# A spare buffer for the blocks that a triangular solve turns, and diagonal copies on three engines, in a hybrid DeltaNet and attention layer

## The chip, the core and the metric

The kernel runs on one core of a Trainium2 chip. A core has five engines that each run a queue of their own in order: TensorE (PE, matrix products; the loads of its weights are listed as PEld), VectorE (DVE), ScalarE (ACT), GpSimd (POOL) and SyncE (SP), which here issues all DMA transfers. Engines wait for each other through semaphores. The metric is the device time of one execution in microseconds; a comparison of two kernels takes the median of several runs of each.

## What is computed

One layer of a bidirectional encoder on x of 2048 rows and 1024 columns, all in float32. The rows are normalised and multiplied by one input matrix, whose columns are split between two groups that are summed at the end:

```python
h = rms_norm(x, norm_w[l])
proj = h @ w_in[l]
dn = gated_deltanet_bidir(dn_q, dn_k, dn_v, dn_beta, dn_decay, ...)   # 4 heads of 128
dn = rms_norm(dn, dn_out_norm_w[l]) * silu(dn_z)
sw = windowed_gqa_with_sinks(sw_q, sw_k, sw_v, ...) * silu(sw_z)      # 8 query heads of 64, 2 key heads
x = x + concat([dn, sw]) @ w_out[l]
```

The gated delta rule, run forward and backward, holds the part that the change touches. In each chunk a unit lower triangular matrix is inverted, and a state is carried from chunk to chunk:

```python
m = where(strict, (k_beta @ k.T) * decay, 0)
t_inv = triangular_solve(eye + m, eye)        # one per chunk
u, w = t_inv @ (v * beta), t_inv @ (k_beta * exp(g))
# scan over the chunks: v_new = u - w @ state; o = ...; state = state * exp(g_last) + k_dec.T @ v_new
```

The reference has chunks of 64; the kernel works the same recurrence in chunks of 128, 16 of them per head and direction.

## The kernel before

The first phase, until about 660 us, makes everything that comes before the recurrence: x is normalised and split into a high and a low part (three products in place of one, hence L191 to L193 and L202 to L204), the projections run, the convolution and SiLU follow (L242, L249), and the windowed attention runs beside them (L343 to L382). Its results go to DRAM: keys and queries per head (kq_d), values (v_d), gates.

The second phase runs over the four heads. Each head goes through four functions, and the work of one head lies beside the scan of the head before it:

- `pre_front(h)`, L637 to L723, in four groups of four chunks: loads keys and queries into a tile of the pool tag "kq", which has two buffers (L654), transposes them on TensorE (L674, tile tr), forms the products of keys with keys and queries (L694, tile gh), scales them on VectorE (L703, tile ma) and writes the triangular matrices to DRAM (L708, m_d).
- `solve(h)`, L725 to L746, inverts the 32 by 32 blocks on the diagonals, 128 of them on 128 partitions, by 31 pairs of VectorE steps: a product into tm (L741), a subtraction from X (L745). L holds the blocks, X starts as the unit matrix, which GpSimd writes by two memsets (L735, L736). The blocks of direction 0 have to be turned: they are loaded into X (L731) and copied, with rows and columns swapped, into L (L734), before X is overwritten. The result goes to DRAM (L746, x_d).
- `invert(h)`, L748 to L796, builds the inverses of the 128 by 128 matrices from the blocks, in four rounds `hi`, each for one group of chunks in both directions. A round loads two pieces of x_d (L757, xc), transposes them on VectorE (L758, xt), adds two matrices into g on GpSimd (L761), and places the 32 by 32 blocks on the diagonals of three operands: e1 by L763, e2 by L765, e3 by L767, four copies each, all on GpSimd. In the trace these operands are iv, and in the order iv0, iv2 and iv3. Five products on TensorE follow (L772, pi0 to pi4), with ScalarE moving their results (L781, b1; L787 to L796), and eight more copies on GpSimd (L784) that place blocks into ma.
- `scan(h)`, L798 to L853, carries the state S through 16 chunks in both directions: a product of the state with the keys (L812, pk), its difference to the values (L814, r), products with the inverse (L821, py), the state's update (L830, L833; L837 is the copy that makes the first state) and the output (L823, L839, L844 to L850, tile oacc). The output's normalisation and gate follow (L864 to L882, tiles sso, tro, zt).

Matmuls that depend on none of this fill TensorE's gaps: 32 pieces of the attention group's output product (L599 to L601, tile pcs, with mxs, mhs, mls as their operands; L602 adds a loaded tile xrs), and some late gate projections (pf_z).

No order is written out by hand. A planner at the end of the build (`set_order`, from L938) takes the instructions, their dependences, a table of costs and lags (L931, L1091) and the pools' number of buffers, runs a list schedule forward and backward twelve times, and fixes the order of all five queues. An edit of a few instructions therefore gives another order in the whole program.

## Time and profile before

| | |
|---|---|
| median of 3 runs | 1278.94 us (1277.84 to 1281.57) |
| the profiled execution | 1274.25 us, its span 1272.5 us |
| mean granted TensorE clock | 0.992 |
| PE busy | 1219.4 us (96%), 7066 matmuls |
| DVE, ACT, POOL busy | 889.5 us (70%), 703.2 us (55%), 507.4 us (40%) |
| DMA | 205.34 MB, mean 161 GB/s |

The span is the time from the first to the last instruction of the profiled execution; the 1.75 us beside it lie around them. An engine's busy time has no waits in it. A share over the whole span hides the stages: until 660 us the first phase runs, from there on the heads. A row of the timeline gives the start, the duration, the engine (SPq is SP's queue of issues), the line, the operation, the output and the inputs, how many of the same kind are taken together, and in brackets how long the engine stood idle before it and what ended that.

### The profile page before, as it was taken

What the parts mean: (1) busy time and instruction counts of PE and PEld (TensorE: products, weight loads), DVE (VectorE), ACT (ScalarE), POOL (GpSimd) and SP (SyncE); (2) the same over time, 40 slices, a digit from 0 to 9 for tenths busy, and PEclk for the clock granted to TensorE, in tenths of its full rate; (3) what the DMA queues carried; (4) which work ended last, traced back from release to release, by engine and by line L of the source; (5) the groups of instructions that cost most, each with busy time, mean ns of one, the idle gap of its engine ahead of it and who ended that gap; (6) DMA issues with size and microseconds to landing.
All of it is one profiled execution on the core that took longest, in us unless ns stands there. A gap on an engine that the chain in (4) does not pass through costs nothing.

```text
span 1272.5 us, 22253 instructions
## 1 busy us (share of the span) xinstructions
PE 1219.4 (96%) x7066; PEld 1044.4 (82%) x7066; DVE 889.5 (70%) x2154; ACT 703.2 (55%) x2105; POOL 507.4 (40%) x893
## 2 busy tenths in 40 slices
PE   6999999999999999999999998998799899999998
PEld 6998877788889998787788787887688789798876
DVE  4422387999975589999986573788488879557333
ACT  6321254776644677776654425858557955566210
POOL 1330044666613398665221306613672651641000
PEclk9999999999999999999999998999899999999999
DMA  8442254322544434522137826967965974746675
GB/s 269 145 132 76 95 180 128 97 97 81 180 132 144 130 96 116 158 87 67 58 117 244 224 96 189 276 189 207 270 169 154 269 191 138 217 145 214 227 242 205
DMA packets 225510, 205.34 MB, mean 161 GB/s; under 512 B 48497, under 2 KB 175089, under 8 KB 225393
## 3 DMA queue, kind: packets, MB, share of 16 engines
q1 hardware_dynamic: 225392, 203.92, 52.7%
q8 instruction: 56, 0.92, 0.3%
q14 instruction: 62, 0.50, 0.1%
HBM read 138.79 MB, written 65.08 MB: 160 GB/s over the span
## 4 chain that ended last, share of the span: by engine, by line
PE 67%; DVE 12%; DMA 9%; ACT 7%; issue 3%; POOL 1%; SPq 0%; DVEq 0%; ACTq 0%; POOLq 0%
PE pf_c L191 4%; PE pf_c L192 4%; PE pf_c L193 4%; PE pf_z L191 4%; PE pf_z L192 4%; PE pf_z L193 4%; PE pi L772 4%; DVE acc L242 3%; PE pt L363 3%; PE pq_q L202 2%; PE pq_q L204 2%; PE pq_q L203 2%; PE pcd L561 2%; PE pcd L563 2%; PE pcd L562 2%
## 5 line engine op out<-in xcount | busy, mean ns | idle before, releaser
L191 PE MATMUL pf_c<-xhi,wh_c 128*128 128x512 f32 x384 | 151.0, 404 | 0.7 <-DVE acc L242 0.4
L192 PE MATMUL pf_c<-xlo,wh_c 128*128 128x512 f32 x384 | 150.6, 401 | 0.0
L193 PE MATMUL pf_c<-xhi,wl_c 128*128 128x512 f32 x384 | 149.1, 401 | 0.0
L242 DVE SCALAR_TENSOR_TENSOR acc<-pf_c,cw,acc 128x512 f32<-128x512 f32 (+1 forms) x192 | 140.3, 743 | 11.3 <-ACT acc L238 9.2
L358 POOL TENSOR_SCALAR pr<-pr,st 128x384 f32<-128x384 f32 (+1 forms) x128 | 80.1, 648 | 71.3 <-DVE st L356 60.0
L191 PE MATMUL pf_z<-xhi,wh_z 128*128 128x512 f32 x256 | 86.6, 401 | 0.5 <-DVE zo L215 0.5
L349 ACT ACTIVATE pr<-pr,st 128x384 f32<-128x384 f32 (+1 forms) x128 | 76.1, 596 | 19.6 <-DVE st L345 19.1
L192 PE MATMUL pf_z<-xlo,wh_z 128*128 128x512 f32 x256 | 86.2, 399 | 0.0
L191 PEld LDWEIGHTS pf_c<-xhi,wh_c 128*128 128x128 f32 x384 | 72.1, 188 | 15.3 <-DVE acc L242 1.7
L193 PE MATMUL pf_z<-xhi,wl_z 128*128 128x512 f32 x256 | 84.7, 397 | 0.0
L192 PEld LDWEIGHTS pf_c<-xlo,wh_c 128*128 128x128 f32 x384 | 72.3, 188 | 13.0
L193 PEld LDWEIGHTS pf_c<-xhi,wl_c 128*128 128x128 f32 x384 | 71.8, 188 | 13.0
L345 DVE CUSTOM_DVE_ANT_0 pr<-s,mask,sink 128x384 f32<-128x384 f32 (+1 forms) x128 | 72.5, 593 | 12.4 <-PE s L344 8.3
L367 ACT ACTIVATE ph<-pt 128x512 fp32r<-128x512 f32 x92 | 53.0, 596 | 40.9 <-PE pt L363 39.1
L826 ACT ACTIVATE yk<-py,ck 128x128 f32<-128x128 f32 x120 | 43.9, 366 | 49.5 <-PE py L821 48.4
L363 PE MATMUL pt<-ident,pr 128*128 128x128 f32 x368 | 67.2, 274 | 1.9 <-DVE q L327 1.1
L368 DVE TENSOR_TENSOR pl<-pt,ph 128x512 fp32r<-128x512 f32 x92 | 61.6, 681 | 5.1 <-ACT ph L367 5.0
L703 DVE SCALAR_TENSOR_TENSOR ma<-gh,bp,dc 128x256 f32<-128x256 f32 x128 | 54.9, 476 | 10.4 <-PE gh L694 8.7
L363 PEld LDWEIGHTS pt<-ident,pr 128*128 128x128 f32 x368 | 46.5, 140 | 17.7 <-DVE pl L368 3.0
L202 PE MATMUL pq_q<-wh_q,xhi 128*128 128x256 f32 x256 | 60.3, 285 | 0.6 <-ACT sgkv L261 0.3
L599 PE MATMUL pcs<-wohs,mhs 128*128 128x512 f32 x128 | 57.7, 451 | 2.9 <-ACT mhs L593 2.3
L814 DVE SCALAR_TENSOR_TENSOR r<-pk,negc,vs 128x128 f32<-128x128 f32 x120 | 41.5, 346 | 27.1 <-PE pk L812 26.6
(251 smaller groups left out, 3709.8 us busy)
## 6 DMA issues: line engine op xcount, KB each, us to landing
kqc<-kq_d SPq DMA_DIRECT2D x120, 128.0 KB, 3.0
ws_c<-wt SPq DMA_DIRECT2D x48, 256.0 KB, 3.3
xr<-x SPq DMA_DIRECT2D x16, 512.0 KB, 6.3
ws_z<-wt SPq DMA_DIRECT2D x32, 256.0 KB, 3.9
kq<-kq_d SPq DMA_DIRECT2D x16, 512.0 KB, 5.3
m_d<-ma SPq DMA_DIRECT2D x32, 256.0 KB, 5.4
mxs<-mix_sw SPq DMA_DIRECT2D x32, 256.0 KB, 3.8
xrs<-x SPq DMA_DIRECT2D x32, 256.0 KB, 3.6
```

The lines of the kernel that those rows point to most:

```text
L191: T.matmul(ps, hi[:, k, cs], xhi[b][:, k], start=(k == 0), stop=False)
L192: T.matmul(ps, hi[:, k, cs], xlo[b][:, k], start=False, stop=False)
L193: T.matmul(ps, lo[:, k, cs], xhi[b][:, k], start=False, stop=(k == KC - 1))
L202: T.matmul(ps[:, :n], xh, hi[:, k, :n], start=(k == 0), stop=False)
L242: V.scalar_tensor_tensor(av, ps[:, lo:], cw[:, i, k : k + 1], av, ALU.mult, ALU.add)
L345: V.tensor_tensor_reduce(pr[j][:, :n], ps[:, :n], mask[:, lo * P : hi * P], 1.0, sink[:, hh : hh + 1], ALU.add, ALU.min, accum_out=nm[:, j ...
L349: A.activation(pr[j][:, :n], pr[j][:, :n], AF.Exp, bias=nm[:, j : j + 1], scale=-1.0, accum_out=den[:, j : j + 1])
L358: G.tensor_scalar(pr[j][:, :n], pr[j][:, :n], den[:, j : j + 1], 1.0, ALU.mult, ALU.mult)
L363: T.transpose(pt[:, j], pr[j][:, (kb - lo) * P : (kb - lo + 1) * P], ident)
L368: V.tensor_tensor(pl, ptf, ph.bitcast(F32), ALU.subtract)
L599: T.matmul(ps, mh[:, k], wh[:, k], start=(k == 0), stop=False)
L703: V.scalar_tensor_tensor(ma[d, c4][:, c], gh[:, k], bp[:, d, cc : cc + 1], gms[d][:, c : c + 1].to_broadcast([P, 2, P]), ALU.mult, ALU.mult,)
```

## The change

Two edits in `solve` and `invert`. In `solve` the blocks of direction 0 are loaded into a new tile lt, which takes a buffer of the "kq" tag, the key tiles of `pre_front`, with still two buffers for that tag. The copy into L reads lt, and stands behind the memsets in the code. In `invert` the copies into e1, e2 and e3 of round 0 go to VectorE, GpSimd and ScalarE, four each; those of rounds 1 to 3 stay on GpSimd. From here on the lines behind the edit have numbers up to three higher (L757 is L759, L758 is L760, L772 is L775; L741 and L745 are L743 and L747; the copies of e1 and e2 are L770, of e3 on ScalarE L768).

```diff
--- before.py
+++ after.py
@@ -728,12 +728,14 @@
         X = qa.tile([P, 32, 32], F32, tag="X", name=f"X{h}")
         lv = [m_d[d].rearrange("u (p y) -> (u p) y", p=4)[:, : 32 * P] for d in range(2)]
         lv = [a.rearrange("q (r x) -> q r x", x=P)[:, :, :32] for a in lv]
-        dma(X[0:64], lv[0])
+        lt = q1.tile([P, 2, 512], F32, tag="kq", name=f"lt{h}", bufs=2).rearrange("p a s -> p (a s)")
+        lt = lt.rearrange("p (r c) -> p r c", c=32)
+        dma(lt[0:64], lv[0])
         dma(L[64:128], lv[1])
         x = X.rearrange("p r c -> p (r c)")
-        V.tensor_copy(L[0:64], X[0:64].rearrange("p r c -> p c r"))
         G.memset(x, 0.0)
         G.memset(x[:, ::33], 1.0)
+        V.tensor_copy(L[0:64], lt[0:64].rearrange("p r c -> p c r"))
         for c in range(31):
             n = 31 - c
             tm = qa.tile([P, 256], F32, tag="tm", name=f"tm{h}_{c}")
@@ -759,12 +761,13 @@
                 x0[d], x1[d] = (xc, xt) if d == 0 else (xt, xc)
             g = qb.tile([P, 4, P], F32, tag="g", name=f"g{h}_{hi}", bufs=2)
             G.tensor_tensor(g, m[:, :, 0], m[:, :, 1], ALU.add)
-            for p, q in enumerate(quads):
-                G.tensor_copy(e1[q, :, q], x0[p % 2][q])
-            for p, q in enumerate(quads):
-                G.tensor_copy(e2[q, :, q], x1[1 - p % 2][q])
-            for p, q in enumerate(quads):
-                G.tensor_copy(e3[q, :, q], x0[p // 2][q])
+            for s, a, b in zip("GGG" if hi else "VGA", (e1, e2, e3), ([0, 1, 0, 1], [1, 0, 1, 0], [0, 0, 1, 1])):
+                xs = x1 if a is e2 else x0
+                for q, k in zip(quads, b):
+                    if s == "A":
+                        A.activation(a[q, :, q], xs[k][q], AF.Copy)
+                    else:
+                        (V if s == "V" else G).tensor_copy(a[q, :, q], xs[k][q])
 
             def prod(j, lhs, rhs):
                 o = ps_i[(hi + j) % 2].tile([P, 4, P], F32, tag="inv", name=f"pi{j}_{h}_{hi}")
```

The planner makes a new order of it. Places of it follow. In names such as `tm1_30_10279` the first number is the head, and the last is a running number of the tile.

VectorE at the end of solve(1), beside the last steps of scan(0) and the products of pre_front(2). Before:

```order
L741 TENSOR_TENSOR tm1_29_10274<-L1_10180,X1_10181 128x60
L685 RECIPROCAL ssk2_11259<-ssk2_11259 128x4
L849 SCALAR_TENSOR_TENSOR oacc0_0_8962<-po0_1_15_9607,egc_4915,oacc0_0_8962 128x128
L745 TENSOR_TENSOR X1_10181<-X1_10181,tm1_29_10274 128x2x30
L703 SCALAR_TENSOR_TENSOR ma2_0_11427<-gh2_0_1_11475,bp2_11261,dc2_0_0_11424 128x2x128
...
L686 TENSOR_TENSOR bp2_11261<-beta_4885,ssk2_11259 128x2x4
L741 TENSOR_TENSOR tm1_30_10277<-L1_10180,X1_10181 128x31
L703 SCALAR_TENSOR_TENSOR ma2_3_11431<-gh2_0_1_11475,bp2_11261,dc2_0_1_11428 128x2x128
L745 TENSOR_TENSOR X1_10181<-X1_10181,tm1_30_10277 128x31
L850 TENSOR_TENSOR oacc0_0_8962<-po0_1_15_9607,oacc0_0_8962 128x128
L849 SCALAR_TENSOR_TENSOR oacc0_3_8975<-po0_0_15_9592,egc_4915,oacc0_3_8975 128x128
```

After:

```order
L747 TENSOR_TENSOR X1_10182<-X1_10182,tm1_29_10276 128x2x30
L836 SCALAR_TENSOR_TENSOR S0_0_14_9561<-S0_0_13_9521,egt_4913,po0_0_14_9553 128x128
L743 TENSOR_TENSOR tm1_30_10279<-L1_10181,X1_10182 128x31
L703 SCALAR_TENSOR_TENSOR ma2_2_11279<-gh2_2_1_11399,bp2_11263,dc2_2_0_11350 128x2x128
L747 TENSOR_TENSOR X1_10182<-X1_10182,tm1_30_10279 128x31
L703 SCALAR_TENSOR_TENSOR ma2_1_11275<-gh2_2_1_11399,bp2_11263,dc2_2_1_11353 128x2x128
L817 SCALAR_TENSOR_TENSOR r0_0_15_9590<-pk0_0_15_9588,negc_4911,vs0_3_8016 128x128
L836 SCALAR_TENSOR_TENSOR S0_1_14_9581<-S0_1_13_9541,egt_4913,po0_1_14_9573 128x128
L852 SCALAR_TENSOR_TENSOR oacc0_3_8976<-po0_0_14_9553,egc_4915,oacc0_3_8976 128x128
...
L817 SCALAR_TENSOR_TENSOR r0_1_15_9605<-pk0_1_15_9603,negc_4911,vs0_0_7950 128x128
L853 TENSOR_TENSOR oacc0_0_8963<-po0_1_14_9573,oacc0_0_8963 128x128
L703 SCALAR_TENSOR_TENSOR ma2_0_11429<-gh2_0_0_11466,bp2_11263,dc2_0_0_11426 128x2x128
```

The last step of solve(1), X1 from tm1_30, stood behind the L703 steps on gh2_0_0 and gh2_0_1 and the scan's r0_0_15, S0_1_14 and r0_1_15; now these stand behind it.

TensorE at the first product of the inverse of head 1, pi0_1_0. Before:

```order
L694 MATMUL gh2_3_0_11540<-kq2_3_11498 128x256 x2
L694 MATMUL gh2_3_1_11551<-kq2_3_11498 128x256 x2
L878 MATMUL tro0_0_9639<-ident_66,oacc0_0_8962 128x128 x4
L878 MATMUL tro0_3_9652<-ident_66,oacc0_3_8975 128x128
L599 MATMUL pcs9_0_11611<-wohs0_9976,mhs9_0_11605 128x512
L600 MATMUL pcs9_0_11611<-wohs0_9976,mls9_0_11606 128x512
L601 MATMUL pcs9_0_11611<-wols0_9977,mhs9_0_11605 128x512
...
L601 MATMUL pcs9_0_11611<-wols0_9977,mhs9_0_11605 128x512
L878 MATMUL tro0_3_9652<-ident_66,oacc0_3_8975 128x128 x3
L772 MATMUL pi0_1_0_10303<-iv0_0_8652,g1_0_10289 128x128 x4
L772 MATMUL pi1_1_0_10318<-b11_0_10308,iv2_0_8655 128x128 x4
```

After:

```order
L694 MATMUL gh2_3_0_11542<-kq2_3_11500 128x256 x2
L775 MATMUL pi0_1_0_10305<-iv0_0_8653,g1_0_10291 128x128 x4
L881 MATMUL tro0_0_9640<-ident_66,oacc0_0_8963 128x128 x2
L694 MATMUL gh2_3_1_11553<-kq2_3_11500 128x256 x2
L775 MATMUL pi1_1_0_10320<-b11_0_10310,iv2_0_8656 128x128 x4
L775 MATMUL pi2_1_0_10327<-iv2_0_8656,b11_0_10310 128x128 x4
L881 MATMUL tro0_0_9640<-ident_66,oacc0_0_8963 128x128
L775 MATMUL pi3_1_0_10336<-iv3_0_8658,g1_0_10291 128x128
L599 MATMUL pcs9_0_11613<-wohs0_9977,mhs9_0_11607 128x512
L600 MATMUL pcs9_0_11613<-wohs0_9977,mls9_0_11608 128x512
L601 MATMUL pcs9_0_11613<-wols0_9978,mhs9_0_11607 128x512
```

The first product has moved ahead of the twelve matmuls of pcs9, of tro0_0 and tro0_3 and of gh2_3_1, which has moved behind it.

VectorE a little later, at the copy that makes the first state of scan(1), S1_0_0. Before:

```order
L758 STREAM_TRANSPOSE xt1_0_1_10349<-xc1_0_1_10348 128x128
L758 STREAM_TRANSPOSE xt1_1_2_10353<-xc1_1_2_10352 128x128
L594 TENSOR_TENSOR mls10_0_11632<-mxs10_0_11626,mhs10_0_11631 128x512
L758 STREAM_TRANSPOSE xt1_0_2_10416<-xc1_0_2_10415 128x128
L602 TENSOR_TENSOR xrs10_0_11635<-xrs10_0_11635,pcs10_0_11637 128x512
L837 COPY S1_0_0_10557<-po1_0_0_10550 128x128
L814 SCALAR_TENSOR_TENSOR r1_0_1_10579<-pk1_0_1_10577,negc_4911,vs1_0_9895 128x128
```

After:

```order
L760 STREAM_TRANSPOSE xt1_0_2_10418<-xc1_0_2_10417 128x128
L602 TENSOR_TENSOR xrs9_0_11611<-xrs9_0_11611,pcs9_0_11613 128x512
L760 STREAM_TRANSPOSE xt1_1_1_10422<-xc1_1_1_10421 128x128
L594 TENSOR_TENSOR mls10_0_11634<-mxs10_0_11628,mhs10_0_11633 128x512
L884 SCALAR_TENSOR_TENSOR zt0_0_9645<-tro0_0_9640,dnw_4875,zt0_0_9645 128x512
L884 SCALAR_TENSOR_TENSOR zt0_3_9658<-tro0_3_9653,dnw_4875,zt0_3_9658 128x512
L840 COPY S1_0_0_10559<-po1_0_0_10552 128x128
L817 SCALAR_TENSOR_TENSOR r1_0_1_10581<-pk1_0_1_10579,negc_4911,vs1_0_9896 128x128
```

The copy stood behind the L602 step of xrs10; that step now stands behind it.

VectorE at the end of scan(2), where the first round of the inverse of head 3 begins. Before:

```order
L745 TENSOR_TENSOR X3_13383<-X3_13383,tm3_30_13479 128x31
L866 TENSOR_SCALAR sso2_1_12661<-ssq2_11262 128x8
L850 TENSOR_TENSOR oacc2_2_12338<-po2_0_11_12588,oacc2_2_12338 128x128
L814 SCALAR_TENSOR_TENSOR r2_1_12_12645<-pk2_1_12_12643,negc_4911,vs2_0_11493 128x128
L833 SCALAR_TENSOR_TENSOR S2_0_12_12636<-S2_0_11_12596,egt_4913,po2_0_12_12628 128x128
...
L833 SCALAR_TENSOR_TENSOR S2_0_13_12722<-S2_0_12_12636,egt_4913,po2_0_13_12714 128x128
...
L758 STREAM_TRANSPOSE xt3_0_0_13484<-xc3_0_0_13483 128x128
L849 SCALAR_TENSOR_TENSOR oacc2_0_12164<-po2_1_13_12734,egc_4915,oacc2_0_12164 128x128
L758 STREAM_TRANSPOSE xt3_1_3_13488<-xc3_1_3_13487 128x128
...
L833 SCALAR_TENSOR_TENSOR S2_0_14_12762<-S2_0_13_12722,egt_4913,po2_0_14_12754 128x128
L758 STREAM_TRANSPOSE xt3_0_1_13551<-xc3_0_1_13550 128x128
```

After:

```order
L747 TENSOR_TENSOR X3_13386<-X3_13386,tm3_30_13483 128x31
...
L817 SCALAR_TENSOR_TENSOR r2_1_12_12648<-pk2_1_12_12646,negc_4911,vs2_0_11495 128x128
L760 STREAM_TRANSPOSE xt3_0_0_13488<-xc3_0_0_13487 128x128
L770 COPY iv0_0_8653<-xc3_0_0_13487 32x4x32 x2
L870 SCALAR_TENSOR_TENSOR sso2_1_12664<-sso2_1_12664 128x8
L760 STREAM_TRANSPOSE xt3_1_3_13492<-xc3_1_3_13491 128x128
L760 STREAM_TRANSPOSE xt3_0_1_13555<-xc3_0_1_13554 128x128
L770 COPY iv0_0_8653<-xt3_1_3_13492 32x4x32 x2
L760 STREAM_TRANSPOSE xt3_1_2_13559<-xc3_1_2_13558 128x128
L836 SCALAR_TENSOR_TENSOR S2_0_12_12639<-S2_0_11_12599,egt_4913,po2_0_12_12631 128x128
```

The transposes of xc3 stood behind the scan's steps S2_0_12 and S2_0_13; now all four, with the four new copies into iv0, stand ahead of S2_0_12.

## The prediction

> **What bounds the kernel now.** I read the span in stretches first, then the waits of TensorE, and then the queues around the longest of those waits. The columns of the first are the stretch, its length, each engine's busy time with its count of instructions (PE, PEld, DVE, ACT, POOL), the granted TensorE clock, the DMA share and GB/s.
>
> ```profile
> 660.00:780.00 120.00, 119.26 (x565) 97.56 (x564) 74.37 (x170) 48.24 (x162) 26.55 (x53) 1.00 0.60 178
> 780.00:830.00 50.00, 42.90 (x274) 38.25 (x273) 31.86 (x79) 40.99 (x158) 29.47 (x56) 0.93 0.93 269
> ...
> 865.00:930.00 65.00, 53.37 (x325) 45.14 (x324) 40.43 (x131) 43.12 (x186) 31.47 (x58) 0.92 0.86 243
> ...
> sum 1272.50, PE 1219.43 PEld 1044.37 DVE 889.51 ACT 703.23 POOL 507.43; mean PE 93.80 PEld 80.34 DVE 68.42 ACT 54.09 POOL 39.03
> ```
>
> TensorE is busy for 1219.4 of 1272.5 us, so 53 us of idle time is all that a change of order can win, and the change touches only some of it. Most of what lies behind the first solve is at two hand-overs from one head to the next: 7.1 us in 780 to 830 and 11.6 us in 865 to 930. Elsewhere TensorE is full (119.3 of 120 us before 780), and work taken off another engine there is worth nothing. A longer stretch ahead of them, which a term below uses:
>
> ```profile
> 45.00:780.00 735.00, 728.80 (x3934) 613.57 (x3935) 540.11 (x1186) 395.99 (x998) 312.53 (x496) 1.00 0.40 123
> ```
>
> The waits that make up the two hand-overs (engine, what waits, for what; us in total, times, longest):
>
> ```profile
> PE tr L674 <- DMA kq<-kq_d: 4.9, 4, 3.9
> PE gh L694 <- DVE ma L703: 3.7, 3, 2.4
> PE pk L812 <- DVE S L837: 2.9, 1, 2.9
> ```
>
> The longest is a load of keys at the first hand-over, the other two lie in the second. What leads up to them there is one chain: the last step of solve(1) on VectorE, its store and re-load, the inverse's first product, the first state of scan(1). VectorE:
>
> ```profile
> 896.72 0.17 DVE L745 TENSOR_TENSOR X<-X,tm 128x31 f32<-128x31 f32 x1
> ...
> 906.74 0.60 DVE L758 STREAM_TRANSPOSE xt<-xc 128x128 f32<-128x128 f32 x2 [1.65 <-DMA xc<-x_d]
> ...
> 922.78 0.69 DVE L602 TENSOR_TENSOR xrs<-xrs,pcs 128x512 f32<-128x512 f32 x1 [4.22 <-DMA xrs<-x]
> 923.39 0.28 DVE L837 COPY S<-po 128x128 f32<-128x128 f32 x1
> ```
>
> SP's queue:
>
> ```profile
> 894.72 0.53 SPq L654 DMA_DIRECT2D kq<-kq_d  x1
> ...
> 897.26 0.64 SPq L746 DMA_DIRECT2D x_d<-X  x1
> ...
> 903.89 0.92 SPq L757 DMA_DIRECT2D xc<-x_d  x2
> ```
>
> TensorE:
>
> ```profile
> 900.71 1.76 PE L694 MATMUL gh<-kq 128*128 128x256 f32 x4 [2.38 <-DVE ma L703]
> ...
> 909.11 1.06 PE L772 MATMUL pi<-iv,g 128*128 128x128 f32 x8
> ...
> 918.27 0.39 PE L821 MATMUL py<-vs,ma 128*128 128x128 f32 x2
> ...
> 923.72 0.49 PE L812 MATMUL pk<-S,kqc 128*128 128x128 f32 x2 [2.94 <-DVE S L837]
> ```
>
> From the store's issue to the first state it takes 26 us (897.26 to 923.39). Of these 6.6 pass between the store's issue and the first load of its data (903.89), and 4.2 to a VectorE step that has nothing to do with the chain: xrs10 (L602) waits for its load until 922.78, and the state's copy is queued behind it.
>
> **The change, part by part.**
>
> *The spare buffer.* The two memsets of X no longer wait for the load and copy of the direction-0 blocks. Before, at solve(1):
>
> ```profile
> 831.97 1.08 DVE L734 COPY L<-X 64x1024 f32<-64x1024 f32 x1
> ...
> 836.49 0.21 DVE L741 TENSOR_TENSOR tm<-L,X 128x31 f32<-128x31 f32 x1
> ```
>
> ```profile
> 833.11 0.95 POOL L735 MEMSET X<- 128x1024 f32 x1 [6.88 <-DVE L L734]
> 834.56 0.82 POOL L767 COPY iv<-xc 32x128 f32<-32x128 f32 x1 [0.50 <-PE pi L772]
> 835.33 0.15 POOL L736 MEMSET X<- 128x32 f32 x1
> ```
>
> Copy, memset, memset and first step stand in a row from 831.97 to 836.49; after, the first step can follow the copy, so up to 3.4 us (836.49 less 833.05) is freed, and at least the memset's 0.95 us. By itself this is worth nothing to TensorE: solve(1) runs from 836.49 to 896.72 beside a scan and filling matmuls. It is worth something only where the solve's end is what the rest waits for, which is the next part. The price is a fifth user per head of the two key buffers: in SP's order the next head's first key load stands behind the new load. For head 3 that is the load at 894.72 above, and its first transpose on TensorE comes 79 us later:
>
> ```profile
> 973.83 0.27 PE L674 MATMUL tr<-ident,kq 128*128 128x128 f32 x1
> ```
>
> Between the two lie the end of solve(1) and its inverse, so the load may slip by tens of microseconds; I cost the move at nothing. The cover is gone if it slips by more than 70, since a key load then takes about 5 us to land and TensorE would stand for what is over.
>
> *What the new order does with solve(1).* By the VectorE order shown with the change, 23 instructions that stood ahead of solve(1)'s last step now stand behind it: nine L703, three scan steps (two L814, one L833), five output steps (L849, L850) and six small ones. An L703 costs 0.42 us (1.25 us for three), an output step 0.33, and I price the scan steps alike and the small ones as the L745 at 896.72, 0.17:
>
> ```profile
> 894.97 1.25 DVE L703 SCALAR_TENSOR_TENSOR ma<-gh,bp,dc 128x256 f32<-128x256 f32 x3
> ...
> 897.01 0.33 DVE L849 SCALAR_TENSOR_TENSOR oacc<-po,egc,oacc 128x128 f32<-128x128 f32 x1
> ```
>
> That is 9 x 0.42 + 8 x 0.33 + 6 x 0.17 = 7.4 us by which the store can leave earlier if VectorE has no waits of its own there. All four xc loads then follow each other on SP, and the state's copy stands ahead of xrs10's step, no longer behind it. On TensorE the first product moves ahead of twelve pcs9 matmuls, eight tro and half of gh2_3. So the chain can win 7.4 us at its head and 4.2 at its end, 11.6 in all, which is also all the idle time of the stretch: the upper bound. The lower bound is a loss: TensorE runs in order, and if the products find no data, what filled 904 to 909 is queued behind them (rival below). DMA argues against the upper end, since it is full here:
>
> ```profile
> 896.00:900.00 4.00, 2.33 (x11) 1.61 (x9) 4.00 (x16) 3.33 (x19) 0.00 (x0) 1.00 1.04 318
> 900.00:904.00 4.00, 2.81 (x8) 1.65 (x8) 2.22 (x7) 1.69 (x8) 2.88 (x2) 0.63 0.93 310
> 904.00:908.00 4.00, 4.00 (x12) 3.12 (x12) 1.52 (x4) 2.10 (x8) 1.11 (x4) 0.51 0.90 219
> ```
>
> A transfer asked for earlier in a full stretch lands not as much earlier. I take half of the bound, -5.5 us.
>
> These windows also show TensorE at half clock, 0.51, behind the gap of 2.38 us: its matmuls there are no idle time, but at a clock of 0.63 and 0.51 the 6.8 us of them cost some 3 us more than at 1.00 (2.81 x 0.37 + 4.00 x 0.49). The Trainium skill ("TensorE: Matmul & The Clock Gate", What's actually happening) puts the fall to half rate behind an idle window of about 3.4 us, on a free-running window; the trace shows it behind 2.38 us already. By the page's length such a gap would cost only itself, and the gain would be nearer -4 than -5.5, the time 1275.9; by the rows, closing it also gives back some of the slow matmuls.
>
> *The diagonal blocks.* In round 0 of each head four copies go to VectorE and four to ScalarE. The nearest rows:
>
> ```profile
> L765 POOL COPY iv<-xt 32x128 f32<-32x128 f32 x28 | 9.5, 338 | 1.2
> ...
> L787 ACT ACTIVATE iv<-pi 32x128 f32<-32x128 f32 x26 | 7.0, 268 | 2.4 <-PE pi L772 2.0
> ```
>
> GpSimd loses 8 x 0.34 = 2.7 us per head; ScalarE gets 4 x 0.27 = 1.1, and VectorE, which shows no such copy, something between 4 x 0.17 (the small L745) and 4 x 0.34; I take the nearer, GpSimd's own. The first product needs e1 and the sum g alone, so at most about 1.4 us (four copies) comes off the chain, and at worst nothing, if the engines hinder each other: the copy at 834.56 above took 0.82 us where the mean is 0.34. I hold this to be inside the -5.5. At head 0 TensorE is full until 780 and then waits for keys, whose load is issued at 784.16 behind five xc loads that held SP:
>
> ```profile
> 765.12 6.30 SPq L757 DMA_DIRECT2D xc<-x_d  x5
> ...
> 784.16 0.56 SPq L654 DMA_DIRECT2D kq<-kq_d  x1
> ```
>
> The load keeps its place in SP's order. Copies done 1 us sooner could free SP 1 us sooner; ScalarE, busy 41 of 50 us here, could lose as much. I take 0, from -1 to +1.
>
> *Head 2.* solve(2) ends at about the same place in VectorE's order. I take -0.5, from -2 to 0, for the start freed and the copies.
>
> *Head 3.* Here the order carries a loss. Thirteen steps that stood ahead of the end of solve(3) now stand behind it (eleven at 0.33 and two like the L602 at 0.69, 5.0 us), but the four transposes and the four new copies are queued ahead of S2_0_12, the step that scan(2) needs. Before, the transposes came 7.7 us after it:
>
> ```profile
> 1080.76 0.18 DVE L745 TENSOR_TENSOR X<-X,tm 128x31 f32<-128x31 f32 x1
> ...
> 1082.39 0.35 DVE L833 SCALAR_TENSOR_TENSOR S<-S,egt,po 128x128 f32<-128x128 f32 x1 [0.55 <-PE po L830]
> ...
> 1090.07 0.30 DVE L758 STREAM_TRANSPOSE xt<-xc 128x128 f32<-128x128 f32 x1
> ```
>
> The way from the last step to the blocks' landing is the landing of a store and then of a load. The first fence is of the stores (L746), the second of the loads (L757):
>
> ```profile
> L746 SPq DMA_DIRECT2D x_d<-X x4: 319/351/635, 760.7 to 1081.0; - x4
> ...
> DMA to landing us min/median/max: 3.2/5.5/6.7
> ```
>
> ```profile
> DMA to landing us min/median/max: 1.9/3.3/5.7
> ```
>
> With 3.2 for the store at its best, 3.3 for the load and the issue of each (0.5) that is 7 us. Against it stand 5 us of steps before the transposes, so VectorE is held for 2 us, and up to 4.5 with the median store (5.5), with scan(2) behind it. TensorE has some filling matmuls, and may not feel it. I take +1.5, from 0 to 4.
>
> *The rest of the plan.* TensorE's order differs from the middle of the first phase on, in small swaps. The stretch 45 to 780 holds 6.2 us of idle time in all. I take 0, from -2 to +2.
>
> The sum is -5.5 + 0 - 0.5 + 1.5 + 0 = -4.5 us. The profiled execution took 1274.25 us, so 1269.75 on its scale; the median of the runs, 1278.94, is 4.69 higher, and on it I forecast 1274.4.
>
> **The rivals.** *Nothing won.* The chain is shorter, but the DMA, at 0.90 to 1.04 from 896 to 908, gives the earlier store and loads the same landing, and only the 4.2 us at xrs10 or less comes free, to be given back at head 3: 1278, within 0.3% (which is also what a measurement can tell from no change, 3.8 us). For it: 6.6 us for the store's landing where 3.2 is possible. Against it: the order moves the store by seven microseconds, not by one.
>
> *Products ahead of their data (slower).* TensorE stands at pi0_1_0 with the pcs9 matmuls, tro and gh2_3_1 behind it. If the blocks land as late as before (906.7), it stands from about 901 until then: the 12 pcs9 (the 12 matmuls in 904 to 908, 2.0 us at full clock) are pushed behind the products, the gap of 2.38 us becomes one of 6, and the 3 us of half clock come again at full price behind it. Price: 2.0 + 3.6 + 3, less the 4.2 won at xrs10: +4.4, 1283. It decides if the store leaves later than about 894, for with 6.6 and 3.3 us of landing the blocks then come after 904, 3 us behind TensorE.
>
> *VectorE's queue at head 3 (slower).* The hold of up to 4.5 us falls on scan(2)'s last steps in full, together with a half-clock stretch of 3 us like that at head 1 behind the gap, while head 1 wins only 3: 1278.94 + 4.5 + 3 - 3 = 1283.4. It decides when the blocks land more than 3 us after the step before the transposes.
>
> *The shared port.* If VectorE's copies shut GpSimd out, e1 and e2 run one after the other as before, and the relief is gone: 1.4 us less, 1275.8. The Trainium skill ("SBUF — State Buffer", Who interferes with whom) says that VectorE and GpSimd lock one port pair for a whole instruction; the 0.82 us copy agrees, and no run here shows eight such copies on the two at once.
>
> **How the numbers follow.** Forecast with gain at the second hand-over: 0.48, the shared port within it or at its edge. Nothing won: 0.22. Products ahead of data: 0.14. Head 3: 0.10. A loss from the other re-planned places, bounded by about 6 us (1285): 0.06. So faster 0.48, same 0.22, slower 0.30. The range reaches from the head-1 bound with 0 elsewhere (1278.94 - 11.6 - 2 for head 2 = 1265) to the slower rivals, 1285. The likeliest case alone spans 1268 to 1275.
>
> **What would show it.** The store x_d of head 1 issued by 892; pi0_1_0 at 904 or so; the state's copy ahead of xrs10's step; in the stretch 865 to 930 idle time down from 11.6 to some 6 us; memsets of X that wait for no copy; round-0 copies on three engines of about 0.27 to 0.3 us. Wrong would be: a gap ahead of pi0_1_0 longer than 2.4 us; a wait of VectorE for xc at head 3 over 3 us; the key load's wait at the first hand-over longer than 3.9 us.

## The result, and the profile after

| | |
|---|---|
| median of 8 runs after | 1286.25 us (1279.98 to 1288.99) |
| median of 8 runs before, same chip | 1278.39 us (1277.32 to 1281.57) |
| ratio | 1.0054, 95% interval 1.0033 to 1.0076 |
| the profiled execution after | 1286.71 us, its span 1284.9 us |

The change makes the kernel 7.9 us slower. The forecast was 1274.4, faster by 4.5 us, and the upper end of its range was 1285.

The span in stretches, of the kernel after (columns as in the prediction):

```profile
165.00:255.00 90.00, 80.95 (x367) 64.10 (x366) 68.29 (x137) 48.72 (x109) 38.72 (x65) 0.98 0.42 137
255.00:660.00 405.00, 398.32 (x2240) 337.93 (x2239) 351.43 (x786) 258.40 (x638) 225.96 (x339) 1.00 0.35 111
660.00:780.00 120.00, 119.95 (x560) 97.72 (x559) 84.29 (x193) 52.62 (x163) 20.56 (x28) 1.00 0.54 166
780.00:830.00 50.00, 42.52 (x253) 35.85 (x252) 29.26 (x75) 37.12 (x150) 33.74 (x74) 0.97 0.80 229
865.00:930.00 65.00, 57.50 (x370) 50.23 (x368) 53.06 (x169) 47.11 (x208) 26.38 (x41) 0.95 0.74 215
```

The first two of them before:

```profile
165.00:255.00 90.00, 87.56 (x414) 70.64 (x413) 76.33 (x157) 52.31 (x117) 46.83 (x78) 1.00 0.45 141
255.00:660.00 405.00, 402.39 (x2261) 340.06 (x2261) 349.74 (x802) 264.15 (x657) 221.97 (x335) 1.00 0.36 111
```

In 865 to 930, where the gain was forecast, TensorE's idle time falls from 11.6 to 7.5 us (7.9 in 882 to 947, where the same work stands in the kernel after, some 17 us late). But in 165 to 255 it rises from 2.4 to 9.0, and in 255 to 660 from 2.6 to 6.7: some 11 us are lost in the first phase, in which the edit touches no instruction. The waits of TensorE after (engine, what waits, for what; us in total, times, longest):

```profile
PE pf_c L191 <- DVE acc L242: 4.6, 2, 3.6
PE pi L775 <- DVE iv L770: 3.9, 2, 3.2
PE tr L674 <- DMA kq<-kq_d: 3.8, 2, 3.6
PE s L343 <- DVE st L345: 3.8, 4, 1.3
```

The waits for keys (4.9 before) and in solve(1)'s chain are still there in part; pf_c and s are products of the first phase.

To see where time is lost, I matched TensorE's instructions of two kernels one by one (the same code line and form, in the same turn) and took the median, over stretches of 15 us of before's time, by how much each starts later. The table is worked out from the starts of one profiled execution each; r9 is the kernel before, profiled once more. Rows between 900 and 990 are left out: there the new order moves products ahead and filling matmuls behind, and a median would mix the two.

```
before's time   after     r1     r2     r6     r7     r4     r9
150               2.3    0.7    0.5    0.9    0.7   -0.3   -0.3
180               8.0    0.7    5.4    0.8    0.5   -0.4   -0.4
210              12.3    1.2    9.7    5.3    0.8   -0.2    0.5
345              12.3    1.2    8.8    5.8    1.2    0.9    0.4
525              16.5    1.6   13.0   11.9    5.7    3.3    0.0
720              14.5    0.7   11.5    9.4    3.4    5.3    0.2
885              17.1    4.2   17.7   13.7    7.7    2.0    2.8
990              12.6    0.4   18.1    8.8    2.0    1.0    2.2
1080             15.2    2.7   19.1    9.8    4.8    1.1    1.5
1260             12.5   -1.2   19.9    5.9    1.2    0.1    2.5
```

After loses in steps: 5.7 us between 150 and 180, 4.3 between 180 and 210, some 4 between 345 and 525; then it wins 4.5 between 885 and 990, where the second hand-over lies. The 2.3 at 150 stand where the order is still the same, and r9 parts from its own kernel by up to 2.8 us around the hand-overs: steps of that size there are chance in one execution, and only the medians can judge them.

### The profile page after: what moved, and what is told of

Read it like the earlier page. It is cut to its first block, busy times and chain, and to the rows that moved or that the text cites. A ratio compares the mean times of both kernels' runs of the same rounds, so it can differ in the third digit from the quotient of the medians.

```text
span 1284.9 us, 22227 instructions
## 1 busy us (share of the span) xinstructions
PE 1220.8 (95%) x7066; PEld 1045.0 (81%) x7066; DVE 898.6 (70%) x2170; ACT 707.4 (55%) x2121; POOL 503.9 (39%) x861
## 4 chain that ended last, share of the span: by engine, by line
PE 66%; DVE 12%; DMA 9%; ACT 7%; issue 3%; POOL 2%; SPq 1%; DVEq 0%; ACTq 0%; POOLq 0%
PE pf_c L191 5%; PE pf_c L192 5%; PE pf_c L193 5%; PE pf_z L191 4%; PE pf_z L192 4%; PE pf_z L193 4%; PE pi L775 3%; DVE acc L242 3%; PE pt L363 3%; PE pq_q L202 2%; PE pq_q L203 2%; PE pq_q L204 2%; PE pcd L561 2%; PE pcd L562 2%; PE pcd L563 2%
## 5 line engine op out<-in xcount | busy, mean ns | idle before, releaser
L242 DVE SCALAR_TENSOR_TENSOR acc<-pf_c,cw,acc 128x512 f32<-128x512 f32 (+1 forms) x192 | 140.1, 743 | 16.9 <-ACT acc L238 13.7
L345 DVE CUSTOM_DVE_ANT_0 pr<-s,mask,sink 128x384 f32<-128x384 f32 (+1 forms) x128 | 72.7, 594 | 5.7 <-PE s L344 4.4
L703 DVE SCALAR_TENSOR_TENSOR ma<-gh,bp,dc 128x256 f32<-128x256 f32 x128 | 55.0, 475 | 16.1 <-PE gh L694 14.1
L183 DVE TENSOR_TENSOR wl_c<-ws_c,wh_c 128x512 fp32r<-128x512 f32 x48 | 38.4, 806 | 32.5 <-ACT wh_c L182 32.2
L203 PE MATMUL pq_q<-wh_q,xlo 128*128 128x256 f32 x256 | 59.7, 283 | 0.0
```

Source lines behind the costliest of these rows:

```text
L203: T.matmul(ps[:, :n], xl, hi[:, k, :n], start=False, stop=False)
L242: V.scalar_tensor_tensor(av, ps[:, lo:], cw[:, i, k : k + 1], av, ALU.mult, ALU.add)
L345: V.tensor_tensor_reduce(pr[j][:, :n], ps[:, :n], mask[:, lo * P : hi * P], 1.0, sink[:, hh : hh + 1], ALU.add, ALU.min, accum_out=nm[:, j ...
L703: V.scalar_tensor_tensor(ma[d, c4][:, c], gh[:, k], bp[:, d, cc : cc + 1], gms[d][:, c : c + 1].to_broadcast([P, 2, P]), ALU.mult, ALU.mult,)
```

## The experiments

All of them compute the whole layer. Each builds the program once without and once with the edits, keeps the two orders that the planner makes (`old`, `new`: numbers of instructions in the order of the code, for each engine), and then hands the planner an order that it must keep, as one more dependence in `set_order`. The first phase are the numbers below 6834, and both programs have the same ones.

```diff
-def set_order(tc):
+def set_order(tc, fixed=()):
...
+    for q in fixed:
+        for a, b in zip(q, q[1:]):
+            started[a].append(b)
```

### Which phase

r1 keeps the edits and the new order of the second phase, with the old order in the first; r17 is the same kernel, run later. r2 has no edit and the old order in the second phase, with the new one in the first.

```diff
+    for e in new:                                                   # r1, r17
+        first = iter([k for k in old[e] if k < 6834])
+        fixed.append([next(first) if k < 6834 else k for k in new[e]])
...
+    fixed = [[k for k in q if k < 6834] for q in new.values()]      # r2
+    fixed += [[k for k in q if k >= 6834] for q in old.values()]
```

> The changed program, all queues in the order of the changed kernel, but the instructions of the first phase (everything before the first head's recurrence) stand among each other as they did in the kernel before. Theory P (the new order of the first phase costs the time; in the second phase the change wins what it was forecast to win, about 2 to 4 us): 1274 to 1277 us. Theory Q (the two profiles of the first phase differ by chance, and the loss comes from the edits and from the second phase): about 1286 us, like the changed kernel.

> The reverse: the program before, without either edit, with the second phase in its own order and the first phase in the order that the changed kernel has. Theory P: the first phase's loss alone, by the two profiles 12 to 14 us less some chance, so 1287 to 1292 us. Theory Q: 1278 us, like the kernel before.

> The kernel with the old first phase and the new second phase once more, beside the one above: 1270 to 1274 us, 0.2 to 0.6% faster than the kernel before.

| median (before, same chip) | first phase old | first phase new |
|---|---|---|
| second phase old, no edit | before: 1278.05 | r2: 1292.2 (1278.05), 1.0116 [1.0097, 1.0134] |
| second phase new, edits | r1: 1272.03 (1278.05), 0.9957 [0.9938, 0.9975]; r17: 1272.6 (1278.73), 0.9948 [0.9932, 0.9964] | after: 1286.25 (1278.39) |

The two effects add: the first phase's new order costs 14.2 us, the second phase wins 6.0, and 14.2 - 6.0 = 8.2 is the loss of 7.9 that was measured. r1 is faster than both kernels.

### A new plan without an edit

r4 has no edit either; the planner's lag for SP is one unit longer, and with that alone it makes another order in both phases.

```diff
-LAG = {"PE": 205, "DVE": 140, "Activation": 160, "Pool": 120, "SP": 2400}
+LAG = {"PE": 205, "DVE": 140, "Activation": 160, "Pool": 120, "SP": 2401}
```

> The kernel before with neither edit; only the planner's lag for SP is 2401 in place of 2400, which gives another order in the first phase and in the second. If any new plan moves the time by several us whatever it is made for: more than 3 us from 1278.4, to either side. If the order only matters where the edits are: 1277 to 1280 us.

1278.75 (1278.05), 1.0003 [0.9987, 1.0019]. A new plan need not cost anything; what the edit drew was a bad one. In the trace r4 loses 5 us in the first phase and has them back at the end.

r9 is the kernel before once more, to see what one execution's chance is.

> The kernel before, unchanged, profiled a second time. Its profiled execution took 1274.25 us where its runs have a median near 1278, so part of what the profiles of two kernels differ by is the chance of one execution. Ratio to the kernel before within 0.15%; if the first profile was a lucky one, this one takes 1276 to 1280 us, and the place where the two part is the size of that chance in a stage.

1277.63 (1277.79), 0.9997 [0.9982, 1.0012], its profiled execution 1276.78 where the first had taken 1274.25: the trace on which the prediction stood was of one of the faster executions.

### The first loss, at 180 us

In both kernels VectorE splits the weights of the convolved projection, in four pieces for each block of 512 columns, from a staging tile ws_c into wl_c (L183), and adds the products pf_c of the block before into acc (L242). A staging tile comes free with its L183 step. VectorE's order before, from row 82 on (weights of the next block, running number 2358; acc steps of the one at work):

```
82 L242 SCALAR_TENSOR_TENSOR acc_0_1626<-pf_c_0_1_1690,cw,acc_0_1626 128x512
83 L183 TENSOR_TENSOR wl_c_0_2358<-ws_c_0_0_2359,wh_c_0_2357 128x2x256
84 L242 SCALAR_TENSOR_TENSOR acc_0_1628<-pf_c_0_1_1720,cw,acc_0_1628 128x512
```

After, the first piece's step stands nine steps later (five of acc, four others), close to the other three of its kind:

```
93 L183 TENSOR_TENSOR wl_c_0_2358<-ws_c_0_0_2359,wh_c_0_2357 128x2x256
94 L249 SCALAR_TENSOR_TENSOR acc_0_1628<-th_0_1756,acc_0_1628 128x1022
95 L183 TENSOR_TENSOR wl_c_0_2358<-ws_c_0_2_2363,wh_c_0_2357 128x2x256
96 L183 TENSOR_TENSOR wl_c_0_2358<-ws_c_0_4_2367,wh_c_0_2357 128x2x256
97 L183 TENSOR_TENSOR wl_c_0_2358<-ws_c_0_6_2371,wh_c_0_2357 128x2x256
98 L242 SCALAR_TENSOR_TENSOR acc_0_2007<-pf_c_0_0_2011,cw,acc_0_2007 128x512
```

In SP's order the load of the third piece (ws_c_0_4_2367, row 112 before) stands behind the store kq_d<-acc (row 112 after), and the fourth behind a second such store. The queue of SP before:

```profile
145.59 15.35 SPq L181 DMA_DIRECT2D ws_c<-wt  x4
164.96 0.34 SPq L251 DMA_DIRECT2D kq_d<-acc  x1
```

and after:

```profile
147.88 5.64 SPq L181 DMA_DIRECT2D ws_c<-wt  x3
166.97 0.34 SPq L251 DMA_DIRECT2D kq_d<-acc  x1
...
169.15 0.38 SPq L181 DMA_DIRECT2D ws_c<-wt  x1
...
170.89 0.38 SPq L181 DMA_DIRECT2D ws_c<-wt  x1
```

SP has issued the last of three loads at 153.52 and then stands 13.4 us at a store, with two loads behind it. VectorE before:

```profile
171.86 0.69 DVE L183 TENSOR_TENSOR wl_c<-ws_c,wh_c 128x512 fp32r<-128x512 f32 x1 [3.06 <-ACT wh_c L182]
172.63 0.75 DVE L242 SCALAR_TENSOR_TENSOR acc<-pf_c,cw,acc 128x512 f32<-128x512 f32 x1
```

and after:

```profile
173.86 0.69 DVE L183 TENSOR_TENSOR wl_c<-ws_c,wh_c 128x512 fp32r<-128x512 f32 x1 [3.04 <-ACT wh_c L182]
178.59 0.69 DVE L183 TENSOR_TENSOR wl_c<-ws_c,wh_c 128x512 fp32r<-128x512 f32 x1 [4.03 <-ACT wh_c L182]
179.37 6.01 DVE L242 SCALAR_TENSOR_TENSOR acc<-pf_c,cw,acc 128x512 f32<-128x512 f32 x9
```

A second wait, of 4.03 us, is new: ScalarE splits the last piece (wh_c) as its load lands,

```profile
177.92 0.63 ACT L182 ACTIVATE wh_c<-ws_c 128x512 fp32r<-128x512 f32 x1 [4.09 <-DMA ws_c<-wt]
```

and nine acc steps are queued on VectorE behind the step that waits for it. They start at 179.37 instead of 172.63, and TensorE has no free PSUM tile for the next pf_c. Its first one before:

```profile
177.72 0.50 PE L191 MATMUL pf_c<-xhi,wh_c 128*128 128x512 f32 x1 [0.45 <-DVE acc L242]
```

and after, with the stretches around it:

```profile
184.12 0.50 PE L191 MATMUL pf_c<-xhi,wh_c 128*128 128x512 f32 x1 [3.58 <-DVE acc L242]
```

```profile
180.00:184.00 4.00, 0.55 (x5) 0.34 (x3) 4.00 (x8) 4.00 (x9) 3.17 (x7) 1.00 0.37 115
184.00:188.00 4.00, 3.88 (x11) 3.11 (x12) 3.88 (x8) 1.16 (x4) 1.00 (x2) 0.65 0.10 10
```

The gap of 3.58 us is followed by a granted clock of 0.65 for 4 us, some 1.4 us more. Which of these moves does it? r3 puts the third piece's load back ahead of the store, r5 also VectorE's first L183 step into its old place:

```diff
+    q = new["SP"]                        # r3, r5
+    q.remove(1838)                       # ws_c_0_4_2367
+    q.insert(q.index(1369), 1838)        # kq_d_87<-acc
+    q = new["DVE"]                       # r5
+    q.remove(1834)                       # wl_c_0_2358, first piece
+    q.insert(q.index(1362), 1834)
```

> The changed kernel in its own order with one instruction moved: on SP the third weight piece ws_c8_4 stands ahead of the store of acc0 again, which it stood behind. If this one load behind a waiting store makes TensorE's waits of 1.1 and 3.6 us for acc at 163 to 184 us, and what follows from them: 1280 to 1282 us. If the loss of the first phase is made of many small moves: 1284 us or more.

> The changed kernel in its own order with two instructions moved: VectorE's step wl_c8_0, whose reading of the staged piece frees the buffer that ws_c8_4 needs, stands ahead of nine VectorE steps again as in the kernel before, and with it the load ws_c8_4 ahead of the store on SP. If the staging of this one weight is the cause of TensorE's wait of 3.6 us at 184 us, that wait goes with the half-clock stretch behind it: 1280 to 1282 us. If not, 1284 to 1287 us.

r3: 1284.22 (1278.05), 1.0051 [1.0033, 1.0070]; r5: 1284.1 (1277.29), 1.0042 [1.0026, 1.0058]. Neither undoes the loss. In r3 the load could leave at 168.34 only, since its staging tile was still held by the L183 step that had moved; in r5 the wait stands too. So whole queues went back to the old order for the part of the first phase that the plan puts ahead of 175 us (in the traces some 185): in r13 those of VectorE and SP, in r18 also ScalarE's, in r6 all five.

```diff
+    until = {"DVE": 175000, "SP": 175000, "all": 0}                              # r13
+    until = {"DVE": 175000, "SP": 175000, "Activation": 175000, "all": 0}        # r18
+    until = {"all": 175000}                                                      # r6
...
+        soon = {k for k in old[e] if k < 6834 and begin[k] < until.get(e, until["all"])}
+        fixed.append((e, [k for k in old[e] if k in soon] + [k for k in new[e] if k not in soon]))
```

> The changed kernel, with VectorE's and SP's queues in the order of the kernel before up to about 185 us; ScalarE, GpSimd and TensorE stay in the new order. If the loss up to there is made in these two queues (weight pieces staged behind steps and a store that wait): as with all queues, 1279 to 1281 us. If ScalarE's or TensorE's order makes it: 1283 us or more.

> The changed kernel, with VectorE's, SP's and ScalarE's queues in the order of the kernel before up to about 185 us; GpSimd and TensorE stay in the new order. If ScalarE's order (the squares of xr ahead of the split of the weight) makes the rest of the loss up to there: 1279 to 1281 us, as with all queues. If TensorE's order makes it: 1282 to 1284 us, as with two.

> The changed kernel, but what the kernel before does in about the first 185 us stands in the order of the kernel before; all that comes later is in the order of the changed kernel. By where the profiles part, 5 to 6 us of the first phase's 14 are lost up to there: 1280 to 1281.5 us. If the loss is spread evenly over the 660 us: 1283 us or more.

r13: 1283.04 (1278.73), 1.0028 [1.0007, 1.0048]; r18: 1279.05 (1278.64), 1.0001 [0.9982, 1.0020]; r6: 1279.75 (1277.29), 1.0002 [0.9983, 1.0022]. TensorE's wait at this place (4.6 us in after) is, in r5, r13, r18 and r6, whose lines are one higher:

```profile
PE pf_c L192 <- DVE acc L243: 4.1, 2, 3.1
```

```profile
PE pf_c L192 <- DVE acc L243: 3.3, 2, 2.7
```

```profile
PE pf_c L192 <- DVE acc L243: 0.9, 2, 0.5
```

```profile
PE pf_c L192 <- DVE acc L243: 0.4, 1, 0.4
```

In r13 VectorE and SP are as before, and the acc steps start at 174.39 again; but one of them then waits for ScalarE. ScalarE, then VectorE in r13:

```profile
180.67 1.06 ACT L147 ACTIVATE xr<-xr 128x1024 f32<-128x1024 f32 x1 [5.79 <-DMA xr<-x]
...
183.07 0.67 ACT L239 ACTIVATE acc<-pf_c,cw 128x512 f32<-128x512 f32 x1
```

```profile
183.77 0.75 DVE L243 SCALAR_TENSOR_TENSOR acc<-pf_c,cw,acc 128x512 f32<-128x512 f32 x1 [4.03 <-ACT acc L239]
```

The new order of ScalarE puts two squares of loaded rows xr ahead of that step of acc, the old one only one. In r18, with the old one, the step starts at 178.53, right behind the first square, and the wait is gone. Of the 4.5 us between the two runs the second square makes 1.4 (181.63 to 183.07); the load of the first landed 3.2 us later in r13 (180.67 against 177.47). The traces show that this too begins on ScalarE: in r13 it splits the third weight piece at 172.41, behind the square that stands before it, in r18 at 164.56; VectorE's step that frees the staging tile follows (173.06 against 169.06); SP waits for that step up to 3.4 us with its next load of a piece, and issues the loads of xr behind it 4.0 us later (174.21 against 170.23). So the new orders of VectorE and SP, taken together, and that of ScalarE each leave a wait here; what VectorE's and SP's would do one by one wasn't tried, beyond the moves of r3 and r5. The intervals of r13 and r18 overlap, so their times alone would not tell them apart; the waits do. All of the step is worth 6.5 us by the medians (1286.25 to 1279.75; in ratios 1.0054 to 1.0002), and 7.0 by the table (12.3 to 5.3 at 210), of which 1.4 stand at 150 already.

### The second loss, at 210 us

In after, VectorE's softmax step of the windowed attention (L345) stands behind acc steps, and TensorE's products s wait for st, 3.8 us in four waits. r7 has the old order in all queues to 235 (by the plan's time), r14 as r6 but VectorE's to 235, r19 as r6 but TensorE's to 235.

```diff
+    until = {"all": 235000}                        # r7
+    until = {"DVE": 235000, "all": 175000}         # r14
+    until = {"PE": 235000, "all": 175000}          # r19
```

> The same up to about 240 us. By the profiles the second place, 205 to 217 us, costs 4 us more, and the rest after it 4 us: 1276 to 1277.5 us. If the loss is spread evenly: 1281 us or more.

> All queues in the old order up to about 185 us, and VectorE's alone up to about 240 us. If the loss at 205 to 217 us comes from VectorE's order (the attention's step L345 behind the convolution's steps): 1275 to 1277 us. If TensorE's or ScalarE's order there makes it: 1279 to 1281 us.

> All queues in the old order up to about 185 us, and TensorE's alone up to about 240 us. If TensorE's order makes the loss at 205 to 217 us: 1275 to 1277 us, as with all queues. If it needs ScalarE's and GpSimd's too: 1278 to 1281 us.

r7: 1275.2 (1277.29), 0.9991 [0.9968, 1.0014]; r14: 1279.17 (1278.73), 1.0000 [0.9982, 1.0018]; r19: 1278.54 (1278.64), 0.9998 [0.9981, 1.0014]. In the table r6 still loses 4.4 us from 180 to 210 and r7 0.3, so the loss is made by orders before 235; in the medians it is 4.5 (1279.75 to 1275.2), in the ratios 1.4 (1.0002 to 0.9991), and the intervals overlap. The ratios of r14 and r19 lie so near both that they don't decide; the traces do. Between 180 and 345 r6 loses 5.0 us by the table's measure, r7 0.7, r14 4.5 and r19 3.3: neither VectorE's order alone nor TensorE's gives it back. The waits for st are no measure of it either: 3.1 us in r6 and 3.2 in r14, which has VectorE's old order, but 1.1 in r19, which still loses. Which set of queues does stays open, as does the rest of the first phase's loss, some 3 us by the medians (r7's 1275.2 to r1's 1272.03; 4.3 by the ratios), which the table puts between 345 and 525 (4.5 in r7, 0.4 in r1).

### What the second phase's gain is made of

The edits without the new order, both and each alone: r8, r11 (spare buffer), r12 (copies). And the new order of the second phase without the edits, on the old first phase: r10. Only the loads into the key tag, and in r10 those into X and its memsets, are left to the planner; the numbers of the copy into L and of the memsets, which change places in the code, are exchanged.

```diff
+    nc, _ = program({'lt': True, 'first': 'VGA'}, old)      # r8
+    nc, _ = program({'lt': True, 'first': 'GGG'}, old)      # r11
+    nc, _ = program({'lt': False, 'first': 'VGA'}, old)     # r12
+    nc, _ = program({'lt': False, 'first': 'GGG'}, new)     # r10, first phase old
```

> Both edits in the kernel before with its own order kept in both phases; only the eight copies that change engine, the new loads and the key loads are placed anew. Theory N (the gain of the second phase comes from its new order, above all the end of solve(1) ahead of the scan's steps): no gain, 1277 to 1280 us. Theory E (it comes from the edits themselves, the memsets that no longer wait and the copies on three engines): 1272 to 1274 us.

> The spare buffer alone, with all else in the order of the kernel before. If it is hidden, as forecast: 1277 to 1279 us. If the fifth user of the key buffers costs something (a key load that comes late at the first or a later hand-over): 1280 us or more.

> The copies on three engines alone, with all else in the order of the kernel before. If they are hidden: 1277 to 1279 us. If VectorE's and ScalarE's copies hold up what is queued behind them (a wait for the blocks' load in front of the scan's steps): 1280 us or more, and then they carry the 2 us that both edits together cost in the old order.

> The kernel before without either edit, its first phase in its own order, its second phase in the order of the changed kernel; only the loads of X and of keys and GpSimd's memsets are placed anew, as the old program needs. Theory N (the new order of the second phase makes the gain of 6 us seen with the old first phase): 1271 to 1275 us. Theory E (the order only pays because the edits make the solves start and the first round's copies end earlier): 1277 us or more.

| | median (before) | ratio |
|---|---|---|
| r8, both edits, old order | 1280.11 (1277.29) | 1.0026 [1.0007, 1.0044] |
| r11, spare buffer, old order | 1281.72 (1277.79) | 1.0022 [1.0003, 1.0041] |
| r12, copies, old order | 1275.48 (1277.79) | 0.9987 [0.9969, 1.0004] |
| r10, new order, no edit | 1276.55 (1277.79) | 0.9993 [0.9977, 1.0009] |

In the old order the spare buffer costs a few microseconds (r11), and the copies win nothing that shows (r12). The new order wins nothing that shows without the edits (r10), and 6.0 us with them (r1, r17): in it the edits are worth 4.5 us (1276.55 to 1272.03), and the interval of r10 meets neither that of r1 nor that of r17. The traces of r10 and r1 show where. TensorE's order is the same in both, and the store of x_d leaves equally early, 3.8 us ahead of the same pcs product (891.84 and 895.67 in r10, 893.43 and 897.28 in r1). But in r10 the first product of the inverse waits for GpSimd, which makes all the copies and has another step between them; TensorE, then GpSimd in r10:

```profile
906.01 2.08 PE L783 MATMUL pi<-iv,g 128*128 128x128 f32 x8 [5.39 <-POOL iv L778]
```

```profile
902.93 0.62 POOL L778 COPY iv<-xt 32x128 f32<-32x128 f32 x2
903.63 1.65 POOL L879 TENSOR_TENSOR sso<-sso,pw 128x8 f32<-128x8 f32 x1
905.34 0.61 POOL L778 COPY iv<-xt 32x128 f32<-32x128 f32 x2
```

With the copies on three engines this wait is 2.62 us in r1 and 3.13 in r17. So the gain is that of the new order together with the copies. No run has the new order with one edit alone, so what the spare buffer does within it is not shown.

In r11 the price that I had put at nothing shows in SP's queue:

```profile
824.57 0.61 SPq L737 DMA_DIRECT2D lt<-m_d  x1
825.27 2.13 SPq L738 DMA_DIRECT2D L<-m_d  x1
827.45 1.48 SPq L655 DMA_DIRECT2D kq<-kq_d  x1
...
832.36 0.55 SPq L655 DMA_DIRECT2D kq<-kq_d  x1
```

In before two loads of keys were issued at 803.5 and 813.8, ahead of the load of the blocks at 826.56; they stand behind the new load now. Whether they alone make r11's loss wasn't separated.

r16 is r1 with one step moved: the last subtraction of solve(1) goes 28 rows back in VectorE's order, behind eight L703 steps and directly behind the one that it followed before.

```diff
+    q = dict(fixed)["DVE"]
+    q.remove(8018)                          # X1<-X1,tm1_30
+    q.insert(q.index(8838) + 1, 8018)       # ma2_3<-gh2_0_1
```

> The kernel with the old first phase and the new second phase (1272 us), with one step moved: the last subtraction of solve(1) stands behind the eight L703 steps of gh2_0 and the scan's steps again, as in the kernel before. If the earlier end of solve(1) makes the gain: 3 to 6 us slower than the next run, 1275 to 1278 us. If the gain comes from elsewhere (head 3, the state's copy ahead of xrs10): within 1.5 us of it.

1278.75 (1278.73), 0.9996 [0.9979, 1.0013], against r17's 1272.6 on the same chip: one step takes the whole gain away. Its first product and the clock behind it in r16:

```profile
909.67 2.05 PE L783 MATMUL pi<-iv,g 128*128 128x128 f32 x8 [9.47 <-DVE iv L778]
```

```profile
908.00:912.00 4.00, 2.33 (x10) 2.02 (x11) 2.92 (x11) 1.60 (x6) 3.48 (x8) 0.50 0.80 253
```

and in r17:

```profile
908.77 1.30 PE L783 MATMUL pi<-iv,g 128*128 128x128 f32 x8 [3.13 <-DVE iv L778]
```

The store of x_d in r16, and in r17:

```profile
899.13 0.33 SPq L755 DMA_DIRECT2D x_d<-X  x1
```

```profile
896.85 0.45 SPq L755 DMA_DIRECT2D x_d<-X  x1
```

In r16 it leaves 3.9 us behind TensorE's first product of the pcs group there (895.25), in r17 3.8 us ahead of the same product (900.69): 7.7 us, where the prediction had worked out 7.4. So the mechanism of the prediction is the one at work (the store of x_d leaves as much earlier as the steps take that now stand behind the last subtraction), and so is its rival: with the products moved ahead and the data not, TensorE stands 9.47 us, and the order turns from a gain to nothing. That xrs10's step stands behind the state's copy was not tried by itself.

## Why the prediction was wrong, step by step

**The step that failed: "The rest of the plan", 0 from -2 to +2.** It measured +14.2 (r2). I had read that TensorE's order differs "from the middle of the first phase on, in small swaps"; in the traces it parts from the old one at 153 us of 660, VectorE's at 160, SP's at 161 and ScalarE's at 164. And I had bounded the term by the 6.2 us of idle time in 45 to 780. Idle time bounds what an order can win. What it can lose has no such bound, since a worse order makes idle time that wasn't there: 6.6 us more in 165 to 255 alone. The rival for this, at 0.06, carried the same wrong bound (6 us, 1285). I had looked at the swaps on TensorE alone; those that make the waits at the first loss are on VectorE, SP and ScalarE. Of the 14.2 us the runs place about half at 180 us (6.5 by the medians) and show how it comes about; for the rest the place is shown and the cause stays open.

**The second hand-over, -5.5: right in mechanism at the head of the chain, and near in size.** The second phase as a whole won 6.0 and 6.1 (r1, r17) where -4.5 was forecast. In after, VectorE's last step, SP's store and loads, and the state read:

```profile
905.30 0.18 DVE L747 TENSOR_TENSOR X<-X,tm 128x31 f32<-128x31 f32 x1
...
916.01 0.31 DVE L760 STREAM_TRANSPOSE xt<-xc 128x128 f32<-128x128 f32 x1 [0.43 <-DMA xc<-x_d]
...
933.81 0.29 DVE L840 COPY S<-po 128x128 f32<-128x128 f32 x1 [2.49 <-PE po L833]
```

```profile
906.36 0.45 SPq L748 DMA_DIRECT2D x_d<-X  x1
...
911.39 3.09 SPq L759 DMA_DIRECT2D xc<-x_d  x4
```

TensorE runs 17.1 us behind before's at 885, so the store at 906.36 is one of 889.3 there, 8.0 us earlier than 897.26 (7.4 worked out, "by 892" asked for). The store's landing came down to 5.0 us (906.36 to 911.39) from 6.6. The idle time of the stretch fell to 7.5 us (7.9 in the stretch 17 us later), not 6. By the table's measure the kernels win 3.8 (r1) and 4.7 us (r17) from 885 to 990, with the edits left out 0.8 (r10), with the subtraction moved back none (r16 loses 1.5), and r9 wins 0.6 by chance. The end of the chain came out otherwise: from the store to the first state it takes 27.5 us (906.36 to 933.81) where it took 26, since filling matmuls now stand between its products, but TensorE no longer waits for the state (pk starts at 934.50 without the 2.94 us of before). That half of an upper bound fits so well is in part luck.

**Products ahead of data, 0.14: half of it came.** I had said that a gap ahead of pi0_1_0 of over 2.4 us would speak against me. It is there, with slow clock behind it:

```profile
918.31 1.37 PE L775 MATMUL pi<-iv,g 128*128 128x128 f32 x8 [3.16 <-DVE iv L770]
```

```profile
918.00:922.00 4.00, 3.44 (x14) 2.80 (x15) 1.63 (x5) 2.63 (x9) 3.63 (x9) 0.63 0.73 236
```

But it is 3.16 us in place of the 6 that this rival worked out, because the store left in time; r16 shows the rival in full.

**Head 3, +1.5: the hazard came and cost nothing that shows.** VectorE does wait for the blocks with scan(2)'s step queued behind:

```profile
1096.14 0.31 DVE L760 STREAM_TRANSPOSE xt<-xc 128x128 f32<-128x128 f32 x1 [1.83 <-DMA xc<-x_d]
...
1098.13 0.30 DVE L836 SCALAR_TENSOR_TENSOR S<-S,egt,po 128x128 f32<-128x128 f32 x1
```

1.83 us of it against the 2 to 4.5 worked out, and in the table after loses nothing there (15.2 at 1080, 12.5 at the end): TensorE had other matmuls.

**The spare buffer "at nothing"** is contradicted by r11 in the old order, by 3.9 us, with an interval that just excludes no change; within the new order it wasn't priced. The memsets wait for no copy any more, as said.

**The copies: right in the old order, too small in the new one.** r12's interval includes no change, as said. In the new order, without them, the first product waited 2.8 us longer (5.39 in r10, 2.62 in r1), twice the 1.4 that I had allowed: I had counted the four copies and not GpSimd's other step of 1.65 us between them. The shared-port rival didn't come. GpSimd and VectorE copy side by side in after:

```profile
916.34 0.61 POOL L770 COPY iv<-xc 32x128 f32<-32x128 f32 x2 [1.72 <-DMA xc<-x_d]
```

```profile
916.25 0.45 DVE L770 COPY iv<-xc 32x128 f32<-32x128 f32 x2
```

**The first hand-over, 0:** the table's 2.6 from 720 to 885 is what r9 shows between two executions of before (2.6); nothing to be read from it. The keys are waited for 3.6 us, against 3.9.

## What to carry to other kernels

Where a planner makes the order, an edit has two prices: its own, and that of the new order wherever the planner draws one, in places that the edit never touches. Bound the second by comparing the queues of all engines from the first row that differs, not by the idle time before, and hold a range for it that reaches as far as whole waits on a queue's head; here it was 14 us of 1278, against 6 won. Keep the old order for the part that the edit doesn't touch, and the gain is there: r1, 1272.03 against 1278.05. And an edit's own price depends on the order it is measured in: the same copies won nothing in the old one.
